# Part two's down products added to part one's by adding transfers into DRAM, and a fourth unit of seven products in step 5 of gate and up

## The chip, the cores and the metric

The kernel runs on one core of a Trainium2 chip (trn2). The metric is the time of one execution on the device, in microseconds. One kernel is one launch; its inputs and its output lie in DRAM. The engines are named as in the profile: PE is TensorE, which multiplies matrices (PEld its loading of weights), DVE is VectorE, ACT is ScalarE, POOL is GpSimd and SP is SyncE. SP computes nothing here: it starts most of the transfers, one after the other in the order of its queue.

## The reference

One layer of an encoder, for 256 tokens of width 2048, in float32: attention in a neighbourhood beside a recurrence, then a feed-forward part, then an embedding for each layer. Cut to what the change touches:

```
def reference(...):
    ...
        h = h + rms_norm(mixed, g_mix_post[i])
        fn = rms_norm(h, g_ffn_pre[i])
        ff = (jax.nn.silu(fn @ w_ffn_gate[i]) * (fn @ w_ffn_up[i])) @ w_ffn_down[i]
        h = h + rms_norm(ff, g_ffn_post[i])
        gate = jax.nn.sigmoid(rms_norm(h, g_ple_pre[i]) @ w_ple_gate[i])
        ple = p[i] @ w_ple_proj[i]
        h = h + rms_norm(gate * ple, g_ple_post[i])
    return h
```

`w_ffn_gate` and `w_ffn_up` are 2048 x 5632 and `w_ffn_down` is 5632 x 2048: 5632 is eleven steps of 512 columns. `mixed` is the output projection of the mixing half (attention and recurrence), whose two halves are normalised each by itself first.

## The kernel before

**One product.** The two operands of every large product are float32. Each is split into two parts in TensorE's own format: ScalarE casts a tile of weights to `wh` (L640), VectorE subtracts `wh` from it and gets `wl` (L653). A product of a block of 128 k by 128 tokens by 512 columns is then three matmuls that add up in one bank: high with high (L691), low with high (L692) and high with low (L693). L702, L703 and L704 are the same three in `product`, which the units below use. The tokens stand as the stationary operand, the weights move.

**The weights.** SP loads a tile of two k blocks of 512 columns (512 KB, L548) into one of four buffers `wr`, or into one more, `third`, in every fifth place. `wh` and `wl` have four buffers and a fifth, for which the buffer of a gain serves in the feed-forward part; the gain is loaded there when that use is over.

**Parts and steps.** The feed-forward part goes in `PARTS` ((0, 4), (4, 8), (8, 11)). For each step f of a part a gate chunk and an up chunk of 512 columns are computed; L1725 and L1744 turn them into a slice of the middle, which goes into `mid` buffers and is then transposed and split (on POOL's or SP's queue, L350 moves `mT`, out of `mid`). Behind a part's steps stand its down products, in two groups of two chunks of 512 output columns (c = 0, 1 and c = 2, 3). Part one's down products are copied to `mid` by ScalarE (L1832) and stored in DRAM by a transfer of POOL (L1835, `part`). For part two POOL first loads what part one left into a `mid` buffer (L1818), VectorE adds the bank to it (L1825), and POOL stores the sum into a second DRAM tile (L1835). Part three begins with the sum of the first two, which SP loads back in two transfers of 1 MB (`reload("mg", t)`, L1848) into the buffers `mg0` and `mg1`.

**Units of seven products.** Two chunks that take the same rows of weights, and a pair of k blocks, are a product of 2 x 2 blocks on either side (two k blocks by two chunks, two token halves by two k blocks). In the plain form that is eight products; a unit does it with seven, after sums of weight blocks and of token blocks. SP loads both tiles of a unit, the first into `wr`, the second into a `lower` buffer. VectorE forms three sums of weight blocks (L588, L592, L598) in `ple`, a buffer that is free until the end of the layer, and POOL adds one more block by an adding transfer (L609). Slots T0 and T1 hold the first tile of sums, in turn, and t0 to t3 the block for the last product; `OUT` gives the block for each t. Of a unit, `four_products` stand first, then (after all four-products of the group, where `made_of_four` combines what the banks hold, L752) `two_products`, and the last products of several units share tiles in `one_product`. Steps f from 2 to 10 have three units each (k pairs 0, 2, 4; `SEVEN_KS`), the down groups of parts one and two four each, and those of part three two each. A unit's first four products are placed between the pairs of the group ahead of it, by the table `FOURS`; `TAKEN` orders the rest inside its own group. The sums of the token blocks are formed once for gate and up, by `sums_of` (L798, L805): for the third pair they lie in the buffer `mg1` until the reload needs it.

**The ring of `lower` buffers.** There are five: slots 0 and 1 are the halves of a tile in the buffer `h0`, slot 2 is a piece of `ple`, slots 3 and 4 are the halves of `lower2`, in the buffer `mg0`. All units in the order of the program take them in turn, the last two excepted:

```
for n, i in enumerate(sorted(lower)):
    lower[i] = (3, 4, 0, 1, 2)[n % RING] if n < len(lower) - 2 else n + 2 - len(lower)
```

The last unit of the gate and up steps has `i == mg1_end`; when its two products are placed, the two reloads are put on the list for 15 and 23 us later in the planner's time.

**The order.** TensorE's order is written out by these tables. The order of everything else comes from `Plan`, a planner that runs when the program is built: streams of tasks (loads, casts, subtractions, sums, what follows a chunk) each give the engine and a cost, the planner keeps a clock for each engine and the times at which buffers come free, and between two products it places those tasks that are due. So the place of an instruction in its engine's queue follows from estimated costs, not from the chip. On the chip every engine, and SP, executes its queue in that order; an instruction that must wait holds all that stand behind it.

**Norms.** In the mixing half four tiles of 128 x 256 are used for the two norms: `ssr` and `ssa` (sums of squares) and an `rb` for each half. They stay allocated to the end.

## Time and profile before

| what | value |
|---|---|
| median of the runs | 1147.19 us (3 runs, 1147.03 to 1148.57) |
| profiled execution, its own time | 1146.92 us |
| its span in the profile | 1145.1 us |
| mean granted TensorE clock | 0.998 |
| PE busy | 1136.3 us, 99% |
| PEld busy | 944.7 us, 82% |
| DVE busy | 932.7 us, 81% |
| ACT busy | 727.2 us, 63% |
| POOL busy | 147.7 us, 13% |
| DMA | 268.49 MB, mean 234 GB/s |

The span runs from the first to the last instruction of the profiled execution; the execution's own time has some 1.8 us more around it. A row of a group names line, engine, operation, output and inputs, shape and count, then busy time and mean in ns of one, then the idle time of the engine just ahead of them with what ended it. `x8: 589/589/590, 570.8 to 612.2` gives shortest, middle and longest in ns, and from which time to which such instructions stand. A row of a timeline begins with the start in us and the duration. In the chain of waits a row is a step of the chain. A row of windows gives the stretch, its length, the busy time and count of each engine in it, the granted clock, the DMA share and GB/s. `SPq` and `POOLq` are the issues of transfers by those engines. A matmul's duration is modelled and overlaps its neighbours', so starts are compared rather than durations.

### The profile page before, as it was taken

The numbers are of one execution on the slowest core, as the hardware profiler recorded it, in microseconds if no ns is written. First come the engines' busy times: TensorE is split into PE (matmuls) and PEld (weight loads), VectorE is DVE, ScalarE is ACT, GpSimd is POOL, SyncE is SP. The second block draws the span as 40 slices with busy tenths as digits, with TensorE's granted clock in tenths as the row PEclk, the third lists the DMA queues.
The fourth block names the chain that finished last, engine by engine and source line by source line (L and its number), as shares of the span: only waits on it lengthen the run. The fifth ranks groups of instructions, "written<-read, shape, count | busy, mean of one in ns | idle before, by whom it ended". The sixth has DMA issues, their size and how long they took to land.

```text
span 1145.1 us, 15184 instructions
## 1 busy us (share of the span) xinstructions
PE 1136.3 (99%) x5193; PEld 944.7 (82%) x5193; DVE 932.7 (81%) x1174; ACT 727.2 (63%) x959; POOL 147.7 (13%) x234
## 2 busy tenths in 40 slices
PE   9999999999999999999999999999999999999997
PEld 8888888888888888888888888888888888788886
DVE  6678697888468779898987898999988888888574
ACT  6877877875447645665666566556555565577564
POOL 0000000000000032132010133222111303100200
PEclk9999999999999999999999999999999999999999
DMA  9867566546685996887977777897797777977861
GB/s 317 295 191 217 182 193 200 175 150 203 220 300 175 314 295 207 228 243 214 292 259 220 257 225 214 249 274 240 257 317 246 216 249 240 278 237 257 240 218 74
DMA packets 110558, 268.49 MB, mean 234 GB/s; under 512 B 36304, under 2 KB 43216, under 8 KB 109072
## 3 DMA queue, kind: packets, MB, share of 16 engines
q1 hardware_dynamic: 96304, 243.17, 63.3%
q0 software_dynamic: 13744, 24.00, 10.9%
q8 instruction: 40, 0.66, 0.2%
q10 hardware_dynamic: 432, 0.35, 0.1%
q14 instruction: 38, 0.31, 0.1%
HBM read 249.65 MB, written 9.44 MB: 226 GB/s over the span
## 4 chain that ended last, share of the span: by engine, by line
PE 93%; DVE 3%; DMA 2%; ACT 2%; issue 1%; SPq 0%; POOL 0%; ACTq 0%; DVEq 0%; POOLq 0%
PE acc L693 23%; PE acc L692 23%; PE acc L691 23%; PE acc L704 6%; PE acc L703 6%; PE acc L702 6%; DVE wl L653 1%; PE tr L331 1%; DMA mg<-part 1%; ACT wh L640 1%; DMA sq<-ev 0%; PE warm L2123 0%; PE pg L362 0%; PE pg L363 0%; PE pg L361 0%
## 5 line engine op out<-in xcount | busy, mean ns | idle before, releaser
L653 DVE TENSOR_TENSOR wl<-wr,wh 128x1024 fp32r<-128x1024 f32 (+1 forms) x300 | 358.6, 1209 | 100.7 <-ACT wh L640 98.9
L640 ACT CAST wh<-wr 128x1024 fp32r<-128x1024 f32 (+1 forms) x300 | 310.8, 1043 | 171.8 <-PE acc L692 114.2
L350 POOL DMA_DIRECT2D mT<-mid x164 | 96.3, 597 | 607.7 <-DMA lower<-in_w_ffn_up 400.7
L692 PE MATMUL acc<-wh,hT_mix_lo 128*128 128x512 f32 x420 | 163.6, 390 | 0.3 <-DVE hT_mix_lo L320 0.3
L691 PE MATMUL acc<-wh,hT_mix_hi 128*128 128x512 f32 x420 | 163.7, 390 | 0.0
L693 PE MATMUL acc<-wl,hT_mix_hi 128*128 128x512 f32 x420 | 163.4, 389 | 0.0
L693 PE MATMUL acc<-wl,hT_hi 128*128 128x512 f32 x320 | 124.6, 390 | 0.0
L691 PE MATMUL acc<-wh,hT_hi 128*128 128x512 f32 x316 | 124.4, 394 | 0.0
L692 PE MATMUL acc<-wh,hT_lo 128*128 128x512 f32 x316 | 123.1, 390 | 0.0
L640 ACT CAST wh<-ple 128x1024 fp32r<-128x1024 f32 (+1 forms) x68 | 68.2, 1008 | 77.2 <-DVE ple L592 47.3
L692 PEld LDWEIGHTS acc<-wh,hT_mix_lo 128*128 128x128 f32 x420 | 78.9, 188 | 17.2 <-DVE hT_mix_lo L320 1.0
L691 PEld LDWEIGHTS acc<-wh,hT_mix_hi 128*128 128x128 f32 x420 | 78.9, 188 | 16.3
L693 PEld LDWEIGHTS acc<-wl,hT_mix_hi 128*128 128x128 f32 x420 | 78.8, 188 | 16.3
L653 DVE TENSOR_TENSOR wl<-ple,wh 128x1024 fp32r<-128x1024 f32 (+1 forms) x68 | 79.2, 1164 | 10.1 <-ACT wh L640 9.7
L693 PEld LDWEIGHTS acc<-wl,hT_hi 128*128 128x128 f32 x320 | 60.1, 188 | 13.0 <-DVE wl L653 0.3
L692 PEld LDWEIGHTS acc<-wh,hT_lo 128*128 128x128 f32 x316 | 59.4, 188 | 11.6
L691 PEld LDWEIGHTS acc<-wh,hT_hi 128*128 128x128 f32 x316 | 59.4, 188 | 11.5
L609 POOL DMA_DIRECT2D ple<-in_w_ffn_up x27 | 24.0, 890 | 164.6 <-DVE wl L653 123.2
L640 ACT CAST wh<-third 128x1024 fp32r<-128x1024 f32 x32 | 33.6, 1051 | 13.4 <-PE acc L692 7.9
L691 PE MATMUL acc<-wh,hT_ffn_hi 128*128 128x512 f32 x104 | 40.9, 393 | 0.0
L692 PE MATMUL acc<-wh,hT_ffn_lo 128*128 128x512 f32 x104 | 40.6, 390 | 0.1
L693 PE MATMUL acc<-wl,hT_ffn_hi 128*128 128x512 f32 x104 | 40.5, 390 | 0.0
(439 smaller groups left out, 2455.6 us busy)
## 6 DMA issues: line engine op xcount, KB each, us to landing
wr<-in_w_in SPq DMA_DIRECT2D x77, 512.0 KB, 4.5
wr<-in_w_ffn_gate SPq DMA_DIRECT2D x73, 512.0 KB, 5.3
wr<-in_w_ffn_down SPq DMA_DIRECT2D x55, 512.0 KB, 6.0
wr<-in_w_ffn_up SPq DMA_DIRECT2D x51, 512.0 KB, 4.8
wr<-in_w_out SPq DMA_DIRECT2D x32, 512.0 KB, 4.3
wr<-in_w_ple_gate SPq DMA_DIRECT2D x32, 512.0 KB, 4.6
lower<-in_w_ffn_up SPq DMA_DIRECT2D x21, 512.0 KB, 6.1
lower<-in_w_ffn_down SPq DMA_DIRECT2D x17, 512.0 KB, 5.5
```

The costliest lines, as they stand in the source:

```text
L331: nc.tensor.transpose(tr[:, b, t * P : (t + 1) * P], e[:, t, sl], ident)
L350: (nc.gpsimd if i in pool else nc.sync).dma_start(dst[32 * j : 32 * j + 32, :, :, i, :], src[32 * i : 32 * i + 32, :, :, j, :],)
L609: nc.gpsimd.dma_start(dst, src, accum_op=ALU.add)
L640: nc.scalar.copy(his[i][:, 0 : src.shape[1], :] if n == 2 else his[i][:, j, :], src)
L653: nc.vector.tensor_tensor(out=los[i][:, m, :], in0=src, in1=f32(his[i][:, m, :]), op=ALU.subtract)
L691: nc.tensor.matmul(accs[t], hi[:, sl], his[i][:, j, :], start=st, stop=False, **group)
L692: nc.tensor.matmul(accs[t], lo[:, sl], his[i][:, j, :], start=False, stop=False, **group)
L693: nc.tensor.matmul(accs[t], hi[:, sl], los[i][:, j, :], start=False, stop=sp, **group)
L702: nc.tensor.matmul(dst, x[0], wh, start=start, stop=False, skip_group_check=seeded)
L703: nc.tensor.matmul(dst, x[1], wh, start=False, stop=False, skip_group_check=seeded)
L704: nc.tensor.matmul(dst, x[0], wl, start=False, stop=stop, skip_group_check=seeded)
```

## The change

Two things are changed, and the buffers for them.

First, part two's down products take the same way as part one's: ScalarE copies them to `mid`, and POOL's transfer adds `mid` to what lies in DRAM (`accum_op=ALU.add`), in one tile `parted` that both parts and the reload use. The load of L1818 and the sum of L1825 are gone.

Second, `FOUR_F = (5,)`: step 5 of gate and up takes its pair k = 6 as a unit too, so it has four units and four plain pairs. The tables get rows for `up4`. The token sums for k = 6 are formed by a further `sums_of` at the end of `more_sums`, into a tile `more` of the tag `quad`; under that tag `quad` stood before, a tile of the same size that now holds the four norm tiles of the mixing half. In a fourth unit (j = 3) the block that `OUT` gives lies below the unit's own slot T1 for odd units, so the two blocks are taken in ascending order, and `turn` says which half each product reads. In the list of weights for the host's layout, k pair 6 of step 5 is stored like those of other units.

With this unit 48 units are in the kernel where 47 were. The formula of the ring of `lower` buffers is not changed.

```diff
+FOUR_F = (5,)
 
 SWAPPED = [
     (lambda f: (("w_ffn_gate", f), ("w_ffn_up", f)), SEVEN_F, SEVEN_KS),
+    (lambda f: (("w_ffn_gate", f), ("w_ffn_up", f)), FOUR_F, (6,)),
...
     TAKEN = {
-        "up3": ("", "01", "2ab"), "down4": ("", "ab0", "12", "3"), "down2": ("", "01", "a"),
+        "up3": ("", "01", "2ab"), "up4": ("", "ab0", "12", "3"), "down4": ("", "ab0", "12", "3"), "down2": ("", "01", "a"),
     }
     FOURS = {
...
+        ("up3", "up4"): (2, 3, 3, 4), ("up4", "up3"): (1, 2, 3), ("up4", "down4"): (1, 2, 3, 3),
+        ("up4", "up4"): (1, 2, 3, 3), ("down4", "up4"): (1, 2, 3, 3), ("up4", "down2"): (2, 3),
...
-            raws[i] = blocks()[:, b0 : b + 1 : b - b0, :]
+            raws[i] = blocks()[:, min(b, b0) : max(b, b0) + 1 : abs(b - b0), :]
...
-        product(C2.accs[0], s["S1"], i, 0, first, last)
-        product(C2.accs[1], s["S2"], i, 1, first, last)
+        turn = int(OUT[j] < 2 - 2 * first_slot[i])
+        product(C2.accs[0], s["S1"], i, turn, first, last)
+        product(C2.accs[1], s["S2"], i, 1 - turn, first, last)
...
         yield from sums_of(hF, 4, t2["s"][:, 0, :], t2["s"][:, 1, :])
+        more = const.tile([P, 4, S], F32R, tag="quad", name="more")
+        yield from sums_of(hF, 6, *(more[:, :, b : b + P] for b in (0, P)))
...
-    ssr = const.tile([P, S], F32, name="ssr")
-    ssa = const.tile([P, S], F32, name="ssa")
+    quad = const.tile([P, 4, S], F32, tag="quad", name="quad")
+    ssr, ssa = quad[:, 0, :], quad[:, 1, :]
...
-        rb = const.tile([P, S], F32, name=f"rb_{name}")
+        rb = quad[:, 2 if name == "rec" else 3, :]
...
-            if part:
-                yield ("pool", COST["move"], None, "mid", None)
-                e, here = mid_tile(), Event()
-                nc.gpsimd.dma_start(e, parts[0].rearrange("t p d -> p t d")[:, :, sl])
-                plan.now += COST["landing"]
-                done(here)
-                yield here
             for t in range(NT):
-                if part:
-                    yield dve(N)
-                    nc.vector.tensor_tensor(
-                        out=e[:, t, :], in0=ch.accs[t], in1=e[:, t, :], op=ALU.add
-                    )
-                else:
-                    yield act(N, take=None if t else "mid")
-                    if not t:
-                        e = mid_tile()
-                    nc.scalar.copy(e[:, t, :], ch.accs[t])
+                yield act(N, take=None if t else "mid")
+                if not t:
+                    e = mid_tile()
+                nc.scalar.copy(e[:, t, :], ch.accs[t])
             ch.release()
             yield ("pool", COST["move"], None, None, None)
-            nc.gpsimd.dma_start(parts[part].rearrange("t p d -> p t d")[:, :, sl], e)
-            plan.now += COST["landing"]
+            to = parted.rearrange("t p d -> p t d")[:, :, sl]
+            if part:
+                nc.gpsimd.dma_start(to, e, accum_op=ALU.add)
+                plan.now += ADDED
+            else:
+                nc.gpsimd.dma_start(to, e)
+                plan.now += COST["landing"]
...
-        nc.sync.dma_start(back[n, t], (spill if n == "h" else parts[1])[t])
+        nc.sync.dma_start(back[n, t], (spill if n == "h" else parted)[t])
...
-                SEVEN_KS if f in SEVEN_F else (),
+                SEVEN_KS + (6,) if f in FOUR_F else SEVEN_KS if f in SEVEN_F else (),
```

More of the change, by code (lines that the diff above doesn't have):

```diff
@@ L786, in sums_of @@
     def sums_of(lhs, kx, hi, lo):
-        lhs.sums[kx] = {
-            n: (hi[:, i * P : (i + 1) * P], lo[:, i * P : (i + 1) * P])
-            for i, n in enumerate(("S1", "S2", "S7", "S4"))
-        }
+        if len(hi.shape) == 2:
+            hi, lo = (x.rearrange("p (b q) -> p b q", q=P) for x in (hi, lo))
+        lhs.sums[kx] = {n: (hi[:, i, :], lo[:, i, :]) for i, n in enumerate(("S1", "S2", "S7", "S4"))}
         yield lhs.ev[kx]
@@ L805, in sums_of @@
             nc.vector.tensor_tensor(out=dst, in0=x, in1=y, op=ALU.subtract)
-        yield from split(hi, lo, f, N, give="T4")
+        yield from split(hi, lo, f.rearrange("p (b q) -> p b q", q=P), N, give="T4")
         done(lhs.ev_sums[kx])
@@ L1611, in layer @@
     ).tile([NT, P, D], F32, name="h_spill")
-    parts = [
-        ctx.enter_context(
-            tc.tile_pool(name=f"parts{i}", bufs=1, space=bass.MemoryType.DRAM)
-        ).tile([NT, P, D], F32, name=f"part{i}")
-        for i in range(2)
-    ]
+    parted = ctx.enter_context(
+        tc.tile_pool(name="parted", bufs=1, space=bass.MemoryType.DRAM)
+    ).tile([NT, P, D], F32, name="parted")
     ev_spilled, ev_all_spilled, ev_back = Event(), Event(), Event()
```

## Prediction

> **What bounds the kernel now.** I read the page first (busy shares, then the chain), next what TensorE waits for, then the stretches around each edit, and last the order of single instructions where transfers and splits meet.

> ```profile
> span 1145.1 us, 15184 instructions
> PE 1136.3 (99%) x5193; PEld 944.7 (82%) x5193; DVE 932.7 (81%) x1174; ACT 727.2 (63%) x959; POOL 147.7 (13%) x234
> PE 93%; DVE 3%; DMA 2%; ACT 2%; issue 1%; SPq 0%; POOL 0%; ACTq 0%; DVEq 0%; POOLq 0%
> ...
> PEld final L2056 <- ACT diag L2054: 2.9, 1, 2.9
> PEld acc L704 <- DVE wl L653: 1.1, 2, 0.6
> ```

> TensorE is busy 99% of the span and makes up 93% of the chain. Of what its weight loads waited for, 2.9 us lie in the last step of the kernel, which the change leaves alone; the 1.1 us behind a split of weights (L653) are the only wait among the products of seven. So time is won by fewer products, and lost where something comes so late that TensorE waits; freeing another engine wins nothing by itself.

> What one product takes is read from the pitch of starts, since the busy time of a matmul overlaps its neighbours'. These two rows of TensorE's timeline stand 24 products apart:

> ```profile
> 981.28 0.39 PE L691 MATMUL acc<-wh,mid2h 128*128 128x512 f32 x1
> 986.72 0.39 PE L702 MATMUL acc<-wh,mid2h 128*128 128x512 f32 x1
> ```

> (986.72 - 981.28) / 24 = 0.2267 us each.

> **Step 5's fourth unit.** A pair of k blocks costs 2 chunks x 2 blocks x 2 token halves x 3 = 24 matmuls in the plain form and 7 x 3 = 21 as a unit. Three go: 3 x 0.2267 = 0.68 us, all of it on the bounding engine. [...]

> The unit is paid by the other engines. Rows by line and form end in the busy time and the mean of one in ns (L609's: shortest, middle and longest, then first start and last end); the windows give length, then busy time and count of PE, weight loads, DVE, ACT and POOL, the clock, the DMA share and GB/s:

> ```profile
> L588 DVE TENSOR_TENSOR ple<-wr 128x512 f32<-128x512 f32 x37 | 25.1, 678 | 0.0
> L592 DVE TENSOR_TENSOR ple<-ple,lower 128x512 f32<-128x512 f32 x38 | 26.2, 690 | 1.2 <-DMA lower<-in_w_ffn_up 0.3
> L598 DVE TENSOR_TENSOR wr<-wr,lower 128x512 f32<-128x512 f32 x31 | 21.2, 685 | 0.0
> L653 DVE TENSOR_TENSOR wl<-wr,wh 128x1024 fp32r<-128x1024 f32 x294 | 354.6, 1220 | 100.5 <-ACT wh L640 98.9
> L653 DVE TENSOR_TENSOR wl<-ple,wh 128x512 fp32r<-128x512 f32 x7 | 4.8, 684 | 0.0
> L609 POOL DMA_DIRECT2D ple<-in_w_ffn_up x27: 850/875/962, 414.3 to 930.9; - x27
> L640 ACT CAST wh<-wr 128x1024 fp32r<-128x1024 f32 x294 | 307.1, 1052 | 171.4 <-PE acc L692 114.2 <-DMA wr<-in_w_in 10.6 <-PE acc L703 10.5
> ...
> 612.00:632.00 20.00, 20.00 (x90) 16.54 (x90) 16.40 (x18) 11.96 (x14) 1.68 (x2) 1.00 0.66 201
> 632.00:652.00 20.00, 20.00 (x90) 16.57 (x89) 15.24 (x17) 10.95 (x13) 1.73 (x2) 1.00 0.94 317
> 652.00:672.00 20.00, 20.00 (x90) 16.58 (x89) 18.20 (x20) 11.31 (x13) 10.29 (x17) 1.00 0.56 146
> 672.00:692.00 20.00, 20.00 (x90) 16.57 (x89) 18.55 (x24) 12.30 (x15) 1.72 (x2) 1.00 0.88 292
> ...
> 648.92 0.68 DVE L752 TENSOR_TENSOR u<-u,acc 128x512 f32<-128x512 f32 x1
> ```

> VectorE gains three sums (0.678 + 0.690 + 0.685 = 2.05 us), three splits of two blocks instead of the two of the plain pair (+1.22), and one more block in the tile of the single products (1.22 - 0.684 = 0.54): 3.81 us. ScalarE gains one cast and half a cast, about 1.5 us. L752 combines a step's first four products; the one at 648.92 is step 5's, so step 4 fills roughly 612 to 652 and step 5 what follows to 692. The sums and the first two splits of the new unit (2.05 + 2.44 = 4.49 us) belong to the end of step 4, where its four products are put between pairs; VectorE then has 16.40 + 15.24 + 4.49 = 36.1 of 40 us. In step 5 the two remaining splits replace those of the pair (-0.7 us), 36.75 becomes 36.1. TensorE is at 20.00 of 20 in stretches where VectorE has 18.55, so this cover holds; without it the sum would lose at most the 4.49 us less the 3.9 idle, 0.6 us. I take nothing.

> The unit also brings one adding transfer on POOL, of the kind that is there already (875 ns of POOL), and takes slots T0, T1 and t3, which the down products use in the same way. Swapping the two products where block 1 lies below block 2 moves no work.

> The sums of the tokens for k = 6, 7 are added at the start of the feed-forward part, by `more_sums`, before the first unit may form.

> ```profile
> L798 DVE TENSOR_TENSOR ple<-hT_mix_hi,hT_mix_lo x6: 412/416/418, 366.2 to 387.1; 128x256 f32<-128x256 f32 x6
> L805 DVE TENSOR_TENSOR ple<-ple x12: 282/284/292, 368.1 to 390.3; 128x128 f32<-128x128 f32 x12
> 366.00:396.00 30.00, 30.00 (x134) 24.85 (x133) 23.03 (x40) 18.41 (x32) 0.00 (x0) 1.00 0.95 295
> ```

> 2 x 0.416 + 4 x 0.284 + one split of 512 (0.69) = 2.66 us of VectorE in a stretch of 30 us with 7 idle, in a row in which the last one today ends at 390.3; the first unit's adding transfer starts at 414.3. Hidden. The norm scratch only puts four small tiles into one of the same size; it adds no instruction, and its reuse waits for reads of the mixing half, long over. Zero.

> **Part two's down products.**

> ```profile
> L1825 DVE TENSOR_TENSOR mid<-acc,mid 128x512 f32<-128x512 f32 x8 | 5.2, 683 | 0.0
> L1832 ACT COPY mid<-acc x8: 589/589/590, 570.8 to 612.2; 128x512 f32<-128x512 f32 x8
> 816.00:836.00 20.00, 20.00 (x90) 16.54 (x90) 19.61 (x24) 11.01 (x12) 2.40 (x3) 1.00 0.85 297
> L1818 POOL DMA_DIRECT2D mid<-part x4: 990/1042/1065, 811.7 to 847.9; - x4
> L1835 POOL DMA_DIRECT2D part<-mid x8: 719/744/1072, 572.3 to 866.1; - x8
> part<-mid POOLq DMA_DIRECT2D x8, 512.0 KB, 6.1
> mid<-part POOLq DMA_DIRECT2D x4, 512.0 KB, 8.8
> 897.84 1.37 ACT L1725 ACTIVATE mid<-acc,rstd_f 128x512 f32<-128x512 f32 x2
> ```

> Eight adds of 0.683 us (5.5 us) leave VectorE, eight copies of 0.589 (4.7 us) join ScalarE, which is busy 11.01 of 20 us there. VectorE is at 19.61 of 20 in this stretch and TensorE still does not wait, so the relief buys nothing. Four loads leave POOL (4 x 1.04 us); four stores become adding transfers. No row has one into DRAM: from 6.1 us (a plain store) to 14.9 (that store after a load, 6.1 + 8.8), I take 9. They wait for copies that stand ahead of them in the old order too; behind them on POOL are the adds of L609, which move forward as the loads ahead are gone. Who waits is the next user of a `mid` buffer: the pair at 866.1 is followed by step 8's gate at 897.84, 32 us later, so even 14.9 us is covered. The reload of the sums comes 100 us later. Zero.

> **Sum.** The profiled execution took 1146.92 us, 1.8 more than its span and 0.27 less than the median of the runs (1147.19). 1146.92 - 0.68 = 1146.24 for such an execution, 1146.5 for the median. That is within 0.2% (2.3 us), about what a measurement of this kernel can tell from no change. This case's own range is 1145.4 (the 1.1 us of L704's waits gone too) to 1148 (the 0.6 above and as much again).

> **Rival: the reload of the sums holds the load queue.** One more unit shifts every later unit by one in the ring of `lower` slots, `(3, 4, 0, 1, 2)[n % RING]`, which excepts only the last two. There were 27 + 16 + 4 = 47 units, now 48. The second unit of part three's first down group was n = 44, slot 2, a piece of `ple`. It becomes n = 45, slot 3: half of `lower2`, whose memory (`mg0`) is where SP reloads the first half of the sums.

> ```profile
> 968.16 0.33 SPq L1848 DMA_DIRECT2D mg<-part  x1
> 974.12 1.64 SPq L548 DMA_DIRECT2D wr<-in_w_ffn_down  x2
> 981.48 0.43 SPq L1848 DMA_DIRECT2D mg<-part  x1
> 983.72 8.10 SPq L350 DMA_DIRECT2D mT<-mid  x8
> ...
> 983.61 0.65 DVE L588 TENSOR_TENSOR ple<-wr 128x512 f32<-128x512 f32 x1
> 985.32 1.22 DVE L653 TENSOR_TENSOR wl<-ple,wh 128x1024 fp32r<-128x1024 f32 x1
> ...
> 981.48 9.73 DMA mg<-part
> 991.23 2.81 DMA mT<-mid
> ...
> 998.77 0.50 PE acc L704
> ...
> 976.00:1000.00 24.00, 23.76 (x103) 19.02 (x103) 20.17 (x23) 12.95 (x15) 5.65 (x9) 1.00 0.93 275
> ```

> That unit's tile is last read by the split at 985.32, done at 986.54. Now the reload goes out at 968.16; then it could not before 986.54, and on SP behind it stand weight loads, the second reload and eight moves of `mT`. This is the one place where the chain leaves TensorE among the products: reload, `mT`, splits, L704 at 998.77, no slack. From the second reload to the last `mT` took 981.48 to 994.04, 12.56 us; from 986.54 that ends at 999.10, 5.1 later, and with another 1024 KB at 275 GB/s (3.8 us) 8.9 later. Less 0.68 that gives 1151.6 to 1155.4. It decides as soon as the wait ends after 981.48, when the second reload goes out today; if part of the loads stands ahead of it, the price can fall to 2 or 3 us. [...]

> Against it: in today's order L588 at 983.61 stands before that split on VectorE and reads a tile whose load (974.12) stands behind the reload on SP. With the wait these would hold each other for ever. So the planner's order there must come out differently, and the diff does not show how; a change that large could also free the reload. Hence below half.

> **Rival: VectorE comes late in steps 4 and 5.** If a split falls behind by one such unit's 4.49 us, TensorE waits between nothing and that, taken as 1 to 4.5: 1146.5 + 1 = 1147.5 to 1151.0. For it: the three old units of the step already stand close together, and the new one's 4.49 us would come on top of them. Against: 19.61 of 20 at 816 without a wait.

> **How the numbers follow.** Hidden, three products fewer: 0.49. Queue held: 0.38. VectorE late: 0.08, half of it beyond 0.2%. Faster by over 2.3 us, which needs a stage to gain that the change does not touch: 0.05; all the waits in the rows above but the last step's come to less. Slower 0.38 + 0.04 = 0.42, same 0.49 + 0.04 = 0.53, faster 0.05. The range runs from the likeliest case's 1145.4 up to 1154.0; it leaves out the faster case and the dearest third of the queue's (0.05 + 0.13 = 0.18).

> **What would show it.** Right: three matmuls fewer, no L1825, TensorE at 20.00 in all stretches from 400 to 980, and the reloads near 968 and 981. The rival: the first L1848 waiting on SP for an L653, `mT` landing near 999 or later, a hole in TensorE after 989. Wrong in my terms: waits for L653 around 612 to 692, or a gate activation waiting for an adding transfer. The forecast fails altogether if the order moves so that another stage begins to wait.

## The result: 0.8% slower, and the profile after

The changed kernel takes 1156.93 us (median of 6 runs, 1156.17 to 1157.20) where the kernel before takes 1147.85 us (6 runs beside it). The ratio is 1.0078, 95% interval 1.0065 to 1.0091: some 9 us slower, above the forecast range's upper end of 1154.0. The profiled execution took 1156.75 us with a span of 1155.0 us, 9.9 us longer than the span before.

The page of the changed kernel, its span and busy times, then the chain by engine:

```profile
span 1155.0 us, 15190 instructions
PE 1139.6 (99%) x5190; PEld 945.7 (82%) x5190; DVE 933.8 (81%) x1177; ACT 732.5 (63%) x969; POOL 147.4 (13%) x231
PE 94%; DMA 2%; DVE 1%; ACT 1%; POOL 0%; issue 0%; SPq 0%; ACTq 0%; DVEq 0%
```

TensorE does three matmuls fewer (5190 for 5193) and yet is busy 3.3 us longer: some of its matmuls have become slower (from 1004.04 to 1008.80 they start 0.42 us apart and more, for 0.2267). The 99% hide the loss. The views that show it are the waits and the windows. What TensorE waits for, then what SP's queue waits for (total, times, longest):

```profile
PE acc L706 <- ACT wh L644: 5.7, 1, 5.7
PE acc L708 <- DVE wl L657: 1.1, 3, 0.6
...
SPq L1843 <- DVE wl L657: 8.6, 1, 8.6
```

(Line numbers are those of the changed kernel: L1843 was L1848, L657 was L653, L644 was L640, L552 was L548, L352 was L350, L342 was L340, L592 was L588, L314 and L316 were L312 and L314, L695 to L697 were L691 to L693, and L706 to L708 were L702 to L704.) The windows of the stretches around the two losses; the count of matmuls stands behind PE's busy time, and the last row is the kernel before:

```profile
670.00:680.00 10.00, 9.42 (x42) 7.50 (x41) 4.90 (x7) 4.93 (x7) 0.99 (x2) 1.00 0.83 212
680.00:690.00 10.00, 9.19 (x41) 7.16 (x39) 9.90 (x13) 6.90 (x8) 0.86 (x1) 1.00 0.51 161
690.00:700.00 10.00, 9.83 (x44) 7.90 (x43) 9.86 (x12) 6.52 (x9) 0.00 (x0) 1.00 0.94 289
...
990.00:1000.00 10.00, 8.36 (x37) 6.57 (x35) 2.88 (x3) 1.06 (x1) 0.87 (x2) 1.00 1.08 291
1000.00:1010.00 10.00, 5.58 (x14) 3.99 (x15) 7.44 (x9) 5.82 (x7) 0.93 (x1) 0.66 0.73 211
...
990.00:1000.00 10.00, 9.76 (x42) 7.44 (x41) 6.60 (x9) 4.94 (x6) 0.94 (x1) 1.00 0.73 196
```

A stretch of 10 us at full pace is counted with 45 or 46 (10 / 0.2267 is 44; those that only reach into it are counted too). Step 5 lacks 4 + 5 + 2 = 11 of them, 11 x 0.2267 = 2.5 us. The 20 us behind 990 lack 9 + 32 = 41, 9.3 us, where the kernel before lacked 4 (0.9 us). So 2.5 + 8.4 - 0.7 for the three matmuls fewer = 10.2 us, near the 9.9 of the spans. There are two losses, and both are real.

**The second one first.** The timelines of SP, of VectorE, of ScalarE and of TensorE around it:

```profile
978.75 0.87 SPq L552 DMA_DIRECT2D wr<-in_w_ffn_down  x1
988.41 0.33 SPq L1843 DMA_DIRECT2D mg<-parted  x1
988.78 0.43 SPq L552 DMA_DIRECT2D wr<-in_w_ffn_down  x1
989.26 0.43 SPq L1843 DMA_DIRECT2D mg<-parted  x1
990.33 10.11 SPq L352 DMA_DIRECT2D mT<-mid  x8
...
985.46 0.65 DVE L592 TENSOR_TENSOR ple<-wr 128x512 f32<-128x512 f32 x1
987.16 1.22 DVE L657 TENSOR_TENSOR wl<-lower,wh 128x1024 fp32r<-128x1024 f32 x1
...
1001.91 1.14 ACT L314 CAST mid2h<-mT 128x512 fp32r<-128x512 f32 x2 [10.84 <-DMA mT<-mid]
...
997.97 0.39 PE L708 MATMUL acc<-wl,mid2h 128*128 128x512 f32 x1
1004.04 0.79 PE L706 MATMUL acc<-wh,sums 128*128 128x512 f32 x1 [5.69 <-ACT wh L644]
...
1006.24 0.63 PE L706 MATMUL acc<-wh,sums 128*128 128x512 f32 x1
1006.66 0.63 PE L707 MATMUL acc<-wh,sums 128*128 128x512 f32 x1
...
1009.57 0.40 PE L695 MATMUL acc<-wh,mid2h 128*128 128x512 f32 x1
```

The first reload goes out at 988.41, three hundredths after the split at 987.16 (done at 988.38) has read the `lower` tile that lies in its memory. Behind it stand a load of weights, the second reload and the eight moves of `mT`. A wait on SP is not a loss by itself: in the same trace loads of weights wait up to 11.6 us for a split; it is the `mT` behind this one that TensorE needs. ScalarE stands 10.84 us at the cast of `mT`, with casts of weights behind it, and TensorE stands still from 998.20 to 1004.04. When it starts again its matmuls come at least 0.42 us apart until 1008.80, and not 0.2267: twelve matmuls from 1004.04 to 1009.57 take 5.53 us instead of 2.72, 0.38 us of it one more wait for a split. So the hole costs about 5.8 us of standing and 2.8 us behind it, nearly all of that slow matmuls.

**The first one.** In step 5 the timelines of ScalarE, VectorE and TensorE show (the first two rows are the kernel before):

```profile
654.81 1.25 DVE L340 STREAM_TRANSPOSE mid<-mid 128x1024 f32<-128x1024 f32 x1
670.81 0.62 ACT L312 CAST mid1h<-mT 128x512 fp32r<-128x512 f32 x1
...
657.61 1.25 DVE L342 STREAM_TRANSPOSE mid<-mid 128x1024 f32<-128x1024 f32 x1
...
676.80 0.62 ACT L314 CAST mid1h<-mT 128x512 fp32r<-128x512 f32 x1 [4.39 <-DMA mT<-mid]
...
677.46 0.69 DVE L316 TENSOR_TENSOR mid1l<-mT,mid1h 128x512 fp32r<-128x512 f32 x1 [5.07 <-ACT mid1h L314]
...
679.34 0.50 PE L708 MATMUL acc<-wl,hT_mix_hi 128*128 128x512 f32 x1 [0.58 <-DVE wl L657]
681.80 0.50 PE L697 MATMUL acc<-wl,hT_mix_hi 128*128 128x512 f32 x1 [0.81 <-DVE wl L657]
```

ScalarE is at the cast of step 4's middle before `mT` has come, and waits 4.39 us; VectorE waits 5.07 us for it; the cast and split of weights that stand behind both are late for TensorE. In the kernel before the same cast started at 670.81 and waited for nothing. Nobody needs this middle before part two's down products. The cast isn't earlier than it was (ScalarE is free for it at 676.80 - 4.39 = 672.41); what it reads is later. The new unit's first four products, 12 matmuls or 2.72 us, stand in step 4, and step 4's middle is transposed 2.80 us later (657.61 for 654.81). Its moves to `mT` also took longer to land, up to 8.5 us for 6.5.

### The profile page after: what moved, and what is told of

Its sections match the earlier page's. It is cut to its first block, busy times and chain, and to the rows that moved or that the text cites. A ratio compares the mean times of both kernels' runs of the same rounds, so it can differ in the third digit from the quotient of the medians.

```text
span 1155.0 us, 15190 instructions
## 1 busy us (share of the span) xinstructions
PE 1139.6 (99%) x5190; PEld 945.7 (82%) x5190; DVE 933.8 (81%) x1177; ACT 732.5 (63%) x969; POOL 147.4 (13%) x231
## 4 chain that ended last, share of the span: by engine, by line
PE 94%; DMA 2%; DVE 1%; ACT 1%; POOL 0%; issue 0%; SPq 0%; ACTq 0%; DVEq 0%
PE acc L697 24%; PE acc L696 24%; PE acc L695 24%; PE acc L708 6%; PE acc L707 6%; PE acc L706 6%; DMA mT<-mid 1%; PE tr L333 1%; DMA mg<-parted 1%; DVE wl L657 1%; POOL mT L352 0%; PE pg L364 0%; PE pg L365 0%; PE pg L363 0%; DMA xs<-in_xT 0%
## 5 line engine op out<-in xcount | busy, mean ns | idle before, releaser
L657 DVE TENSOR_TENSOR wl<-wr,wh 128x1024 fp32r<-128x1024 f32 (+1 forms) x301 | 360.0, 1209 | 99.5 <-ACT wh L644 95.2
L644 ACT CAST wh<-wr 128x1024 fp32r<-128x1024 f32 (+1 forms) x301 | 311.4, 1043 | 163.6 <-PE acc L696 107.5
L352 POOL DMA_DIRECT2D mT<-mid x164 | 96.5, 605 | 609.8 <-DMA wr<-in_w_ffn_gate 400.7
L697 PE MATMUL acc<-wl,hT_mix_hi 128*128 128x512 f32 x416 | 162.0, 389 | 0.8 <-DVE wl L657 0.8
L695 PE MATMUL acc<-wh,hT_mix_hi 128*128 128x512 f32 x416 | 162.1, 390 | 0.0
L697 PE MATMUL acc<-wl,hT_hi 128*128 128x512 f32 x320 | 124.5, 390 | 0.0
L695 PE MATMUL acc<-wh,hT_hi 128*128 128x512 f32 x316 | 124.4, 394 | 0.0
L644 ACT CAST wh<-ple 128x1024 fp32r<-128x1024 f32 x69 | 70.2, 1021 | 74.1 <-DVE ple L596 50.0
L697 PEld LDWEIGHTS acc<-wl,hT_mix_hi 128*128 128x128 f32 x416 | 78.1, 188 | 17.2 <-DVE wl L657 1.2
L695 PEld LDWEIGHTS acc<-wh,hT_mix_hi 128*128 128x128 f32 x416 | 78.1, 188 | 16.1
L657 DVE TENSOR_TENSOR wl<-ple,wh 128x1024 fp32r<-128x1024 f32 x69 | 81.2, 1180 | 8.4 <-ACT wh L644 8.1
L697 PEld LDWEIGHTS acc<-wl,hT_hi 128*128 128x128 f32 x320 | 60.1, 188 | 12.8
L695 PEld LDWEIGHTS acc<-wh,hT_hi 128*128 128x128 f32 x316 | 59.4, 188 | 11.4
L644 ACT CAST wh<-third 128x1024 fp32r<-128x1024 f32 x33 | 34.8, 1054 | 19.6 <-PE acc L696 12.6
L657 DVE TENSOR_TENSOR wl<-third,wh 128x1024 fp32r<-128x1024 f32 x33 | 40.2, 1219 | 4.1 <-ACT wh L644 3.7
L695 PE MATMUL acc<-wh,hT_ffn_hi 128*128 128x512 f32 x104 | 40.9, 393 | 0.1
## 6 DMA issues: line engine op xcount, KB each, us to landing
wr<-in_w_ffn_gate SPq DMA_DIRECT2D x78, 512.0 KB, 5.4
wr<-in_w_in SPq DMA_DIRECT2D x77, 512.0 KB, 4.5
wr<-in_w_ffn_down SPq DMA_DIRECT2D x57, 512.0 KB, 5.9
wr<-in_w_ffn_up SPq DMA_DIRECT2D x43, 512.0 KB, 4.9
wr<-in_w_out SPq DMA_DIRECT2D x32, 512.0 KB, 4.4
wr<-in_w_ple_gate SPq DMA_DIRECT2D x32, 512.0 KB, 4.4
lower<-in_w_ffn_up SPq DMA_DIRECT2D x23, 512.0 KB, 6.3
third<-in_w_ffn_up SPq DMA_DIRECT2D x17, 512.0 KB, 4.8
```

The costliest lines, as they stand in the source:

```text
L352: (nc.gpsimd if i in pool else nc.sync).dma_start(dst[32 * j : 32 * j + 32, :, :, i, :], src[32 * i : 32 * i + 32, :, :, j, :],)
L644: nc.scalar.copy(his[i][:, 0 : src.shape[1], :] if n == 2 else his[i][:, j, :], src)
L657: nc.vector.tensor_tensor(out=los[i][:, m, :], in0=src, in1=f32(his[i][:, m, :]), op=ALU.subtract)
L695: nc.tensor.matmul(accs[t], hi[:, sl], his[i][:, j, :], start=st, stop=False, **group)
L697: nc.tensor.matmul(accs[t], hi[:, sl], los[i][:, j, :], start=False, stop=sp, **group)
```

## The experiments

The theory after the result: the shared slot holds SP's queue (8 us), and one cast too far ahead in ScalarE's queue for its late `mT` loses step 5 (2.5 us). Rivals: the reload's place in the queue, VectorE having too much to do, the adding transfers themselves. All medians stand beside runs of the kernel before on the same chip.

**The adding transfers alone.**

```diff
-FOUR_F = (5,)
+FOUR_F = ()
...
-        more = const.tile([P, 4, S], F32R, tag="quad", name="more")
-        yield from sums_of(hF, 6, *(more[:, :, b : b + P] for b in (0, P)))
```

> Only the adding transfers; step 5 has three units, 47 units in all, the ring as before. The reload of the first half of the sums stands right ahead of the second here, as in the changed kernel, and not three loads earlier as in the kernel before. Theory 1 (the 8 us behind 998 come from the shared slot: the reload waits for the split of a unit in the same memory): no unit holds mg0 that late, so the reload goes out near 979 and the time is the kernel before's within 0.5 us. Rival 2 (the 8 us come from the reload's new place in SP's queue, with both reloads back to back ahead of mT): mT lands 3 to 6 us later relative to its transposition and the time is 2 to 5 us above before. Rival 3 (the adding transfers themselves hold a mid buffer or POOL): waits behind 866, the gate activation of step 8 after its time, +1 to +3 us.

1148.47 us, ratio 1.0012 (1.0003 to 1.0021). No wait of 8 us, nothing in step 5. But SP's timeline, which had the reloads at 968.16 and 981.48 before, shows the planner's new order:

```profile
977.98 0.41 SPq L1841 DMA_DIRECT2D mg<-parted  x1
981.09 0.43 SPq L1841 DMA_DIRECT2D mg<-parted  x1
```

(L1841 here is L1843 of the changed kernel.) So it is the adding transfers that put the first reload 10 us later, though part two's down products lie 100 us ahead of it. By itself that costs little: 0.6 us by the medians, a hair more than the 0.5 that theory 1 allowed, and the interval reaches from 0.3 to 2.4 us.

**The whole change, the ring turned.**

```diff
-        lower[i] = (3, 4, 0, 1, 2)[n % RING] if n < len(lower) - 2 else n + 2 - len(lower)
+        lower[i] = (3, 4, 0, 1, 2)[(n + 4) % RING] if n < len(lower) - 2 else n + 2 - len(lower)
```

> The whole change, but the ring of lower slots starts four places further, so that the last down units have slots 1, 2, 0, 1 and not 2, 3, 0, 1: nothing in mg0 behind step 10. Theory 1: L1843 no longer waits 8.6 us, goes out near 980, mT lands some 10 us behind its transposition as before, and 8.0 us come back: 1.9 us above before (0.68 won, 2.6 lost in step 5). Rival 2 (place in the queue): half or less comes back, 4 to 8 us above before.

1151.03 us, ratio 1.0027 (1.0015 to 1.0038): 5.9 us of the 9.1 come back, between what the two theories said. SP, TensorE and the windows there:

```profile
980.40 1.00 SPq L1843 DMA_DIRECT2D mg<-parted  x1
984.12 0.43 SPq L1843 DMA_DIRECT2D mg<-parted  x1
...
1001.05 0.50 PE L706 MATMUL acc<-wh,sums 128*128 128x512 f32 x1 [1.54 <-ACT wh L644]
...
990.00:1000.00 10.00, 9.51 (x42) 7.53 (x41) 4.24 (x5) 3.00 (x5) 2.03 (x4) 1.00 1.03 202
1000.00:1010.00 10.00, 8.08 (x34) 6.18 (x35) 9.88 (x12) 6.99 (x8) 1.68 (x2) 1.00 0.75 224
```

The reload waits no longer, and the granted clock stays at 1.00. 4 + 12 = 16 matmuls are missing, 3.6 us, 2.7 more than before: what the late place of the reload costs together with the rest of the order, which was not taken apart here. The slot's own part is then 8.4 - 2.7 = 5.7 us, the slow matmuls included. Step 5's loss stays (3 + 9 + 2 matmuls missing from 670 to 700).

**Four units alone**, with the ring turned and part two's down products the old way (load, VectorE's add, store).

```diff
-                nc.gpsimd.dma_start(to, e, accum_op=ALU.add)
+                nc.gpsimd.dma_start(e, parts[0].rearrange("t p d -> p t d")[:, :, sl])
...
+                    nc.vector.tensor_tensor(
+                        out=e[:, t, :], in0=ch.accs[t], in1=e[:, t, :], op=ALU.add
+                    )
```

> Four units in step 5 with the ring turned by four; part two's down products go the old way (load, VectorE add, store). If the 2.6 us in step 5 come from the fourth unit alone: TensorE waits near 678 to 692 as in the changed kernel, 1.9 us above before, and mT near 994 as before. If they need the adding transfers (by another order of the planner): 0.7 us below before.

1150.12 us, ratio 1.0020 (1.0010 to 1.0029), 2.3 us above before, near the 1.9 expected. ScalarE waits 4.80 us for `mT` at 677.70 in step 5, and the reload goes out at 970.65, in its old place. The loss in step 5 belongs to the fourth unit, the place of the reload to the adding transfers. Four units alone on the ring as it stands were not tried.

**The cast later.**

```diff
-            plan.add(carried(mid, kk0, mT), plan.now + (0.5 if soon else {0: 12.0, 9: 6.0}.get(f, 3.0)), -SOON if soon else 0.0)
+            plan.add(carried(mid, kk0, mT), plan.now + (0.5 if soon else {0: 12.0, 4: 9.0, 9: 6.0}.get(f, 3.0)), -SOON if soon else 0.0)
```

> The whole change, but the cast of step 4's middle is put on the list 9 us and not 3 us behind the planned landing of mT. Theory A (the 2.6 us in step 5 are one cast that stands at the head of ScalarE's queue and waits 4.4 us for mT, with casts and splits of weights behind it): the wait goes, 2 to 2.6 us come back, 1154.5 where the changed kernel has 1156.9. Rival B (VectorE has too much to do in steps 4 and 5 with the unit's 3.8 us): its work is unchanged, so the loss stays and the time is 1156.9 within 0.5. The hole behind 998 stays in both.

1156.22 us, ratio 1.0072 (1.0059 to 1.0084). The median moved 0.7 us where theory A expected 2 to 2.6, and the interval overlaps that of the changed kernel, so what the wait costs in time is left open by this run. The profiled execution shows the mechanism; its span is 2.2 us shorter (1152.8), but it is the fastest of the five (1154.57 us, the others 1155.97 to 1156.76). ScalarE's cast, then the windows:

```profile
679.46 0.61 ACT L314 CAST mid1h<-mT 128x512 fp32r<-128x512 f32 x1
...
670.00:680.00 10.00, 10.00 (x46) 8.28 (x45) 8.21 (x9) 6.74 (x8) 1.44 (x2) 1.00 1.05 290
680.00:690.00 10.00, 10.00 (x46) 8.25 (x45) 9.72 (x12) 6.97 (x9) 0.86 (x1) 1.00 0.59 174
690.00:700.00 10.00, 10.00 (x46) 8.29 (x45) 9.36 (x12) 5.89 (x8) 1.21 (x2) 1.00 0.72 257
```

The cast finds `mT` there, all 46 matmuls are in each stretch, with VectorE's work unchanged: rival B, VectorE too full for the unit in step 5, is out.

**All three mended**: ring, cast, and the first reload earlier.

```diff
-            plan.add(reload("mg", 0), plan.clk["pe"] + 15.0)
+            plan.add(reload("mg", 0), plan.clk["pe"] + 11.0)
```

> The whole change with three edits: the ring turned by four, the cast of step 4's middle 9 us and not 3 us behind the planned landing, and the first reload put on the list 11 us and not 15 us behind the last product of step 10, so that it stands three loads earlier, as in the kernel before. If slot, cast and place of the reload are all that the change loses: no wait of over 0.6 us among the products, and the time is 0 to 0.7 us below before (three products fewer), which cannot be told from no change. If the adding transfers themselves cost something: 0.5 to 1.5 us above before.

1148.07 us, ratio 1.0001 (0.9992 to 1.0009): the time of the kernel before is back. The gain of 0.68 us cannot be seen; the stretch 990 to 1000 still lacks 9 matmuls (2.0 us), 5 more than before.

```profile
990.00:1000.00 10.00, 8.58 (x37) 6.49 (x36) 5.55 (x7) 4.29 (x7) 0.30 (x1) 1.00 0.71 188
```

**The adding transfers alone, the reload early** (the first and the last of these diffs together).

> The adding transfers alone, and the first reload three loads earlier, as in the kernel before. If the 0.6 us of the adding transfers alone (0.86 us of it one wait for a split at 998) come from the two reloads standing back to back: that wait falls to 0.2 us and the time is before's within 0.4 us. If they come from the adding transfers: it stays 0.6 to 1.4 us above before.

1147.34 us, ratio 0.9995 (0.9986 to 1.0004): with the early reload the adding transfers cost nothing that can be measured. The small wait for L657 near 998 did not fall as expected (0.84 for 0.86 us), so what exactly the early place saved here stays open.

**The hole filled.** In front of the products that wait until 1004, TensorE adds zeros to a bank that is being filled:

```diff
+        if group is groups[-1] and j == 0:
+            hi = group.lhs.at[0][0]
+            for _ in range(46):
+                nc.tensor.matmul(groups[-2].chunks[0][0].accs[0][0:64, 0:S], zeros, hi, start=False, stop=False, skip_group_check=True)
```

> The whole change, and in front of the product that waits until 1004 TensorE does 46 matmuls of 64 x 256 by zeros, which add nothing to a bank that is being filled: 46 x 0.113 = 5.2 us of work in a hole of 5.7 us. If the slow matmuls behind the hole (12 products in 5.5 us where 2.7 are usual, granted clock 0.66) come from TensorE having stood idle: they keep a pitch of 0.23 us and 2.4 us come back, 1154.5 where the changed kernel has 1156.9. If they come from the weights or the transfers at that time: 1156.9 as before, within 0.5.

1154.25 us, ratio 1.0064 (1.0050 to 1.0078): 2.7 us less than the changed kernel by the medians, though the two intervals overlap; span 1152.5 for 1155.0, with the reload as late as in the changed kernel (988.45). TensorE's timeline and window (this kernel's L708 and L697 are L706 and L695 of the changed one):

```profile
998.24 5.53 PE L732 MATMUL acc<-mid2h,zeros 128*64 128x256 f32 x46
1003.61 0.40 PE L708 MATMUL acc<-wh,sums 128*128 128x512 f32 x1
1007.23 0.39 PE L697 MATMUL acc<-wh,mid2h 128*128 128x512 f32 x1
...
1000.00:1010.00 10.00, 9.40 (x57) 7.85 (x56) 8.25 (x11) 6.07 (x7) 0.93 (x1) 1.00 0.78 245
```

The same twelve matmuls take 3.62 us instead of 5.53, a wait of 0.60 us in them, and the granted clock stays at 1.00, with the moves of `mT` as late as they were (990.37 for 990.33). The slow matmuls came from TensorE having stood still.

**More fourth units.** If the cast's place were the unit's only price, more of them would win. With the three edits of above and other steps in `FOUR_F` (and the cast of the middle of the step ahead of each later):

```diff
-FOUR_F = (5,)
+FOUR_F = (5, 7, 9)
```

> As the version with all three edits, but with four units in steps 5, 7 and 9, and the casts of the middles of steps 6 and 8 put later too: six more products fewer, 3 x 0.68 = 2.0 us in all. If the cast's place in the queue is the only price of a fourth unit: 1.5 to 2.0 us below before. If VectorE (3.8 us more in each of the three) comes late: each such step loses 1 to 2.6 us, 1 to 5 us above before.

1147.83 us, ratio 1.0002 (0.9994 to 1.0011): the time of the kernel before, with nine matmuls fewer. The stretch behind 990 is whole here, but a new gap stands behind step 7:

```profile
780.00:790.00 10.00, 9.27 (x41) 7.38 (x40) 9.77 (x11) 5.30 (x7) 4.69 (x8) 1.00 0.58 111
790.00:800.00 10.00, 8.90 (x39) 7.03 (x39) 8.96 (x11) 5.56 (x7) 0.93 (x1) 1.00 0.77 231
...
990.00:1000.00 10.00, 10.00 (x46) 8.29 (x45) 8.96 (x11) 5.33 (x7) 4.05 (x7) 1.00 0.85 207
```

5 + 7 = 12 matmuls, 2.7 us, more than the 2.0 won. Without step 7, with others in its place, and with more:

```diff
-FOUR_F = (5,)
+FOUR_F = (3, 5, 9)
```

> As the version with four units in steps 5, 7 and 9, but in 3, 5 and 9, with the casts of the middles of steps 2, 4 and 8 put later. Step 7 is followed by part two's down products; there the version with 5, 7, 9 lost 12 products' time (2.7 us) between 780 and 800, and nothing near 998. If that loss belongs to step 7 alone: 2.0 us below before, no stretch of 10 us with fewer than 45 matmuls between 400 and 1040. If each fourth unit only moves the loss to another place: before's time within 0.7 us.

1152.65 us, ratio 1.0037 (1.0025 to 1.0049). A split that TensorE waits 2.76 us for at 549.

```diff
-FOUR_F = (5,)
+FOUR_F = (5, 6, 9)
```

> The same with steps 5, 6 and 9 (casts of the middles of steps 4, 5 and 8 later). Nine products fewer as well: 2.0 us below before if neighbouring steps can both have the unit; if VectorE, 3.8 us more in each of two steps in a row, comes late: before's time or up to 2 us above.

1155.94 us, ratio 1.0062 (1.0048 to 1.0075). One split is 6.86 us late at 773, and the clock falls again behind it:

```profile
773.01 0.79 PE L708 MATMUL acc<-wl,s 128*128 128x512 f32 x1 [6.86 <-DVE wl L657]
...
760.00:770.00 10.00, 6.15 (x28) 4.75 (x26) 2.83 (x3) 2.00 (x2) 3.87 (x6) 1.00 1.01 268
770.00:780.00 10.00, 6.99 (x21) 5.55 (x22) 8.78 (x10) 5.14 (x7) 0.88 (x1) 0.66 0.51 143
```

VectorE is busy 2.83 us of 10 there: it is not full, it stands.

```diff
-FOUR_F = (5,)
+FOUR_F = (3, 4, 5, 6, 8, 9)
```

> Four units in steps 3, 4, 5, 6, 8 and 9: 18 products fewer, 4.1 us. If VectorE, at 9.0 to 9.9 of 10 us in these stretches, can hold it: 3 to 4 us below before. If it is full: splits come late, TensorE waits for L657 in most of these steps, and the time is before's or 1 to 5 us above.

1158.79 us, ratio 1.0100 (1.0087 to 1.0113). TensorE waits for splits of L657, 4.3 us in all at L708 (two waits, the longest 2.7) and 2.8 us in all at L697 (four), with the gap at 549 as in the version with 3, 5, 9. VectorE's busy share is 82%, so whether it was full in single steps or its queue in a bad order was not separated here.

```diff
-FOUR_F = (5,)
+FOUR_F = (5, 9)
```

> As the version with four units in steps 5, 7 and 9, without step 7, whose fourth unit was followed by a loss of 2.7 us at 780 to 800: six products fewer than before. If steps 5 and 9 keep their good order: 1.4 us below before. The planner's order changes with each unit, so the loss may appear elsewhere, as it did with 3, 5, 9 and 5, 6, 9: then before's time or up to 5 us above.

1150.20 us, ratio 1.0023 (1.0014 to 1.0032). No gap at 780, but a wait stands in TensorE's timeline for a part of step 9's middle (step 10's is transposed only at 986.91):

```profile
984.60 0.50 PE L696 MATMUL acc<-wh,mid2l 128*128 128x512 f32 x1 [2.56 <-DVE mid2l L316]
```

None beats the kernel before. The gaps move with the set of steps, but ahead of those at 549, 773 and 984 the trace shows what it showed in step 5, ScalarE standing at the cast of a middle: step 3's for 2.34 us until 545.22 (units in 3, 5, 9) and for 2.29 us until 545.46 (in six steps), step 9's for 2.99 us until 978.86 (5, 9), and step 6's for 8.42 us until 770.48 (5, 6, 9), where VectorE stands 8.30 us behind it. No run moved these casts, so that they are the cause there too is not shown.

## Why the prediction was wrong

**Three matmuls, 0.68 us: right**, by their count. **Part two's down products, zero: right for the transfers themselves.** With the reload in its old place they cost nothing measurable (1147.34 us, ratio 0.9995); that they would move the reload in the planner's order was not in the working. Stores and adding transfers together landed in 7.1 us (median), the adding ones alone in 7.7, between the plain store's 6.1 and the 9 taken. POOL takes 1.22 us to issue one, not 0.75:

```profile
parted<-mid POOLq DMA_DIRECT2D x8, 512.0 KB, 7.1
...
L1830 POOL DMA_DIRECT2D parted<-mid x4: 740/748/754, 572.4 to 613.2; - x4
L1827 POOL DMA_DIRECT2D parted<-mid x4: 1205/1216/1223, 821.8 to 862.6; - x4
```

**The fourth unit's work in steps 4 and 5, "I take nothing", at most 0.6 us: the step that failed first.** I summed VectorE's busy time and asked whether it was full. The sum was about right (VectorE is busy 1.1 us longer in all, and 3.81 + 2.66 - 5.5 makes 1.0), and it was not full; it stood 5.07 us with work behind the instruction that waited. The working counted what the unit's first four products add to step 4 for VectorE, and not that they put off the end of step 4, and with it `mT`, by 2.8 us. It named no instruction that waits for a transfer at the head of ScalarE's or VectorE's queue, though the moves of `mT` lay in that stretch of the trace. The rival "VectorE comes late" had the size (1 to 4.5, measured 2.5 by the count of matmuls) with the wrong mechanism; its sign, waits for the split L657 between 612 and 692, is there at 679.34 and 681.80.

**The reload behind the shared slot: the rival, put at 0.38, was what happened**, with its wait and its place; without step 5's loss the profiled execution would stand at 1156.75 - 2.5 = 1154.3, inside the 1151.6 to 1155.4 given for that case. It was put below half because the reload ahead of the load that L588 needs would hold for ever, and the order "must come out differently". It did: the adding transfers moved the reload behind that load (L588, now L592, reads its tile at 985.46, and the reload goes out at 988.41), which makes the wait possible without freeing the reload. I took the unknown order as a chance of escape; it was only what let the wait be. This is the second step that failed, and the dearer one: it left some 8.4 us out of the likeliest case because the order had to change.

But the price was made of other parts than the sum said. The 5.1 to 8.9 us of later landing were all to be standing. The cast of `mT` started 7.8 us later than before (1001.91 for 994.14), but 1.8 of that the kernel was late by then already (2.5 - 0.7), and the standing was 5.8 us. The 2.8 us behind it, nearly all slow matmuls, were not in the sum at all. That the total still lies in the range of that case is in part luck. The rows show how slow the matmuls were: behind 5.8 us and 6.86 us of standing the matmuls start 0.42 us apart or more where 0.2267 is usual, for 4.8 us in both; in the changed kernel the granted clock is 0.50 in every stretch of 1 us from 1004 to 1008, and 1.00 from 1009 to 1010.

**The range.** I treated the two losses as cases of which one would come true, and let the range end inside the dearer. They add: 1146.92 - 0.68 + 2.5 + 8.4 = 1157.1 us, against 1156.75 for the profiled execution. (The 2.5 and 8.4 are counted after the result, so this checks the account and is no forecast.)

## What to carry to other kernels

When an edit changes how many tiles go round a ring of shared buffers, write down which tile gets which memory afterwards and who overwrites it next: here a reload that waited 8.6 us for that memory held the ten transfers behind it in SP's queue. An engine's busy share does not say whether a piece of work is covered (VectorE, busy for 81% of the span, stood 5.07 us with work behind it): look for the instruction at the head of its queue that waits for a transfer, at what stands behind it, and at whether the change puts off what the transfer carries. Price a hole in TensorE's work with the slow matmuls behind it (2.8 us, nearly all of that slow matmuls, behind 5.8 us of standing here), and add the prices of rivals that do not exclude each other.

## What the runs showed of the hardware

```profile
549.22 0.50 PE L708 MATMUL acc<-wl,mid0h 128*128 128x512 f32 x1 [2.76 <-DVE wl L657]
...
550.00:560.00 10.00, 10.00 (x39) 8.10 (x38) 9.35 (x11) 4.22 (x4) 0.86 (x1) 0.85 0.72 247
```

Small matmuls that add zeros, 64 x 256 where the real ones are 128 x 512, were enough here to keep the clock up: 1.00 from 1000 to 1010 with 5.53 us of them in the hole, where 0.66 stood without.
